# A table of 476 moves applied to the instruction order of a two-layer hybrid decoder trunk

## The chip, the cores and the metric

The kernel runs on one core of one Trainium2 chip. The metric is the device time of one execution in microseconds (us), lower is better. The core has five instruction queues that matter here: TensorE (PE in the profile, with its weight loads as PEld), VectorE (DVE), ScalarE (ACT), GpSimd (POOL) and SyncE (SP), which issues all the transfers between DRAM and on-chip memory. Each queue runs its instructions in the order in which they are written; between queues there are semaphores.

## The reference

```python
D_MODEL, SEQ, DEPTH, D_FF = 1024, 1024, 2, 2816
def reference(x, ...):
    for l in range(DEPTH):
        h = rmsnorm(x, attn_norm[l])
        c_q, c_kv, k_r, g_b, g_c, u_conv, u_pool, q_sw, k_sw, v_sw = split(h @ w_in[l])
        y_a = mla_attention(c_q, c_kv, k_r, ...)       # 4 heads, causal
        y_b = short_gated_conv(g_b, g_c, u_conv, conv_w[l])
        y_c = multiscale_pool(u_pool, ...)
        y_d = swa_sink_attention(q_sw, k_sw, v_sw, ...)  # window 128
        mixed = rmsnorm_of_each_group(y_a, y_b, y_c, y_d) * mix_norm[l]
        x = x + mixed @ w_o[l]
        h2 = rmsnorm(x, ffn_norm[l])
        gate, up = split(h2 @ w_gate_up[l])
        x = x + (silu(gate) * up) @ w_down[l]
    return rmsnorm(x, final_norm)
```

All of it is float32, with one sequence of 1024 tokens.

## The kernel before

The activations lie transposed: channels on the 128 partitions, tokens on the free axis, in two halves of 512 tokens. Each float32 operand of a matmul is split into a high part in a reduced format (`fp32r`, a cast on ScalarE, line 280) and the rest (a subtraction on VectorE, line 283), and each product is the sum of three matmuls (high x high, high x low, low x high; `mm3`, line 260). So every weight that is loaded passes through ScalarE and VectorE before TensorE can use it.

A layer has four stages, in the time of layer 0: attention and the other mixers with the input projection (0 to about 352 us), the output projection and the second norm (to about 430 us), gate and up of the FFN (to about 880 us), and the down projection (to about 1160 us); layer 1 follows in the same way.

The two products of the FFN are done as 2 x 2 blocks with seven block products instead of eight, so weights and activations are first added to one another: the weights on POOL (lines 1213 to 1215 and 1243 for gate and up, line 1532 for down), the activations on VectorE. In the FFN a step `f` computes one column block of gate and up for all tokens: it loads two pieces of `w_gu` (lines 1202 and 1204), adds and splits them, and runs seven groups of 12 or 24 matmuls into banks of PSUM. VectorE and ScalarE take the results out of the banks: line 1333 (gate = bank + snapshot), line 1321 (a snapshot of a bank, on ScalarE), line 1658 (`up`), line 1670 (the second half of the gate), line 359 (times the norm's factor), line 1453 (silu on ScalarE, followed by a product on POOL, line 1454), line 1447 (`neg_mul`, the finished activation, which reads the bank last and so gives it back to TensorE). Lines 1132, 1463 and 1465 combine finished activations, and line 1468 stores them. At some steps the weights of the down projection are also prepared (load, line 1525; sums on POOL, line 1532; store, line 1535).

In the stage between, `out_last` (line 1181) adds the output projection to the residual, and `rnorm` ends the norm: line 351 is an exponential on ScalarE, line 352 a product on VectorE, behind which TensorE starts the next product. Lines 1143, 1145 and 1153 (`combine`) prepare block sums of the activations there. In attention, line 466 is a split for the sliding-window queries and keys, line 634 the sliding-window product with the values.

The order of the instructions is not that of the code. The kernel is traced once; the class `Order` then has a planner with a cost for each kind of instruction, which simulates the five queues and puts the instructions of each queue in a row (`find`, `run`). The row is imposed on a second trace as dependencies between neighbours (`impose`). The names of tiles in the order carry a number; `u` are the slots in SBUF, `ps_` the banks in PSUM, `te`, `tn`, `tp` temporary tiles, `in_` inputs in DRAM, `ad`, `qd`, `gd` scratch in DRAM.

Of the kernel before, what the change touches and what calls it, by code (L numbers as in the profile page):

```python
# [1801 lines left out]

class Order:


# [202 lines left out]
    def banks(self, end):  # L2010
# [11 lines left out]
            given.append(b)  # L2022
        return given

    @staticmethod
    def impose(tc, traced, order):
        for ks in order.values():
            for a, b in zip(ks, ks[1:]):
                tc.add_manual_dep(
                    traced[b],  # L2030
                    traced[a].name,
                    mybir.DependencyInfo(
                        mybir.DependencyClass.NoSync, mybir.DependencyReason.DATA
                    ),
                    reason="order",
                )


def scheduled_kernel(fresh, ins_of, rounds=4):

    def trace(banks, order=None):
        nc = fresh()
        ins, out = ins_of(nc)
        with tile.TileContext(nc) as tc:
            trunk_kernel(tc, ins, out, banks)
            traced = [
                i
                for i in nc.cur_bb.bb.instructions  # L2050
                if Order.queue(i) in Order.ENGINES and i.opcode != "TilePoolBoundary"
            ]
            if order is not None:
                Order.impose(tc, traced, order)
        return nc, traced

    nc, traced = trace(None)
    plan = Order(traced, nc.dependency_edges)
    best = None
    for _ in range(rounds):  # L2060
        banks = plan.banks(plan.find()[2])
        nc, traced = trace(banks)
        plan = Order(traced, nc.dependency_edges)
        found = plan.find()
        if best is None or found[0] < best[0]:
            best = found[0], banks, found[1]
    return trace(best[1], best[2])[0]


def _constants():  # L2070
# [130 lines left out]
```

## Time and profile before

| | |
|---|---|
| median of 3 runs | 2066.03 us (2065.02 to 2066.41) |
| span of the profiled execution | 2061.2 us |
| granted clock of TensorE | 1.00, by stretches 0.99 to 1.00 |
| instructions on PE, DVE, ACT, POOL | 9422, 2443, 1743, 420 |
| moved by transfers | 302.37 MB |

The profiled execution has a span only, from its first instruction to its last; no device time of that same execution is given beside it. Its times by stages (stretch: length, then busy us and count of PE, PEld, DVE, ACT and POOL, granted clock of TensorE, mean busy share of the DMA engines, GB/s):

```profile
0.00:352.00 352.00, 348.33 (x1712) 284.49 (x1713) 302.03 (x690) 217.61 (x484) 14.11 (x28) 1.00 0.26 89
352.00:430.00 78.00, 74.20 (x323) 59.34 (x323) 70.86 (x108) 58.80 (x91) 4.11 (x2) 1.00 0.36 127
430.00:1170.00 740.00, 737.13 (x3316) 608.70 (x3315) 492.49 (x677) 296.65 (x468) 281.12 (x191) 1.00 0.50 168
1170.00:1380.00 210.00, 209.37 (x1042) 171.31 (x1041) 185.97 (x418) 140.56 (x309) 2.95 (x16) 1.00 0.23 77
1380.00:1445.00 65.00, 63.36 (x278) 51.67 (x277) 61.89 (x95) 51.59 (x80) 5.78 (x2) 1.00 0.32 113
1445.00:2061.00 616.00, 602.95 (x2760) 498.05 (x2758) 390.49 (x456) 227.38 (x317) 269.28 (x183) 0.99 0.54 183
```

To read it: the length of a stretch less the busy time of PE is the time in which TensorE did nothing there.

### The profile page before, as it was taken

Reading aid. Unit: us, or ns where it says so; the run is one execution under the profiler, and the core shown is the slowest. Engines: PE = TensorE matmul, PEld = TensorE weight load, DVE = VectorE, ACT = ScalarE, POOL = GpSimd, SP = SyncE. Lnnn points to the kernel's source line nnn. Section 1 sums busy time; section 2 is a strip of 40 time slices with the busy share of each in tenths; the row PEclk is TensorE's granted clock in tenths of the full one; section 3 lists DMA queues with packets and bytes.
Section 4 is the critical chain, followed back from the end, with each engine's and each line's share of the span. In section 5 each row is a group of like instructions: output and inputs, shape, how many; then the busy total and the mean of one; then the engine's idle time right before and its main releaser. Section 6 shows DMA issues by size and latency. Waiting matters only on the chain.

```text
span 2061.2 us, 26597 instructions
## 1 busy us (share of the span) xinstructions
PE 2035.3 (99%) x9422; PEld 1673.6 (81%) x9422; DVE 1503.7 (73%) x2443; ACT 992.6 (48%) x1743; POOL 577.3 (28%) x420
## 2 busy tenths in 40 slices
PE   9999999999999999999999999999999999999998
PEld 7887888778888888888888878888788877788887
DVE  8779979987666667655657898889866655585555
ACT  7447657753333334444433666668433333354342
POOL 0200000037777773000002000000577777710000
PEclk9999999999999999999999999999999999999999
DMA  5211223334554556766413112142455555487642
GB/s 191 90 57 46 84 78 96 137 133 168 181 175 167 189 169 235 265 220 208 140 46 124 37 42 97 61 144 94 159 169 178 178 175 170 154 302 237 204 171 96
DMA packets 142118, 302.37 MB, mean 147 GB/s; under 512 B 13856, under 2 KB 60960, under 8 KB 141984
## 3 DMA queue, kind: packets, MB, share of 16 engines
q1 hardware_dynamic: 141984, 300.66, 43.1%
q8 instruction: 74, 1.21, 0.2%
q14 instruction: 60, 0.49, 0.1%
HBM read 212.00 MB, written 87.56 MB: 145 GB/s over the span
## 4 chain that ended last, share of the span: by engine, by line
PE 68%; POOL 7%; DVE 5%; DMA 4%; issue 2%; ACT 2%; SPq 0%; DVEq 0%; POOLq 0%; ACTq 0%
PE ps_mm L260 25%; PE ps_s L260 21%; PE ps_t L260 8%; PE ps_pv L260 6%; POOL u L1532 3%; PE ps_pv L1044 2%; PE ps_t L1032 1%; DMA u<-in_w_dn 1%; POOL tp L1454 1%; DMA ad<-u 1%; POOL u L1214 1%; DVE u L283 1%; POOL u L1213 1%; ACT u L280 1%; DMA u<-in_w_gu 1%
## 5 line engine op out<-in xcount | busy, mean ns | idle before, releaser
L260 PE MATMUL ps_mm<-u,u 128*128 128x512 f32 (+1 forms) x3378 | 831.0, 390 | 3.4 <-ACT u L280 2.3
L260 PEld LDWEIGHTS ps_mm<-u,u 128*128 128x128 f32 x3378 | 615.4, 188 | 130.4 <-issue 5.3
L260 PE MATMUL ps_s<-u,u 128*128 128x512 f32 x2670 | 636.1, 390 | 5.8 <-DVE tn L352 2.3
L283 DVE TENSOR_TENSOR u<-u,u 128x1024 fp32r<-128x1024 f32 (+2 forms) x400 | 443.3, 1126 | 225.2 <-ACT u L280 173.4
L260 PEld LDWEIGHTS ps_s<-u,u 128*128 128x128 f32 x2670 | 499.5, 188 | 117.8 <-ACT tn L1321 3.9
L280 ACT CAST u<-u 128x1024 fp32r<-128x1024 f32 (+2 forms) x400 | 345.1, 881 | 505.4 <-POOL u L1215 60.1
L260 PE MATMUL ps_t<-u,u 128*128 128x512 f32 (+1 forms) x1124 | 255.3, 378 | 2.8 <-DVE u L1447 2.7
L260 PEld LDWEIGHTS ps_t<-u,u 128*128 128x128 f32 x1124 | 201.6, 188 | 45.8 <-DVE u L1447 6.5
L1454 POOL TENSOR_TENSOR tp<-tp,u 128x512 f32<-128x512 f32 x80 | 135.1, 1689 | 341.7 <-ACT tp L1453 341.7
L260 PE MATMUL ps_pv<-u,u 128*128 128x512 f32 x744 | 177.8, 390 | 1.6 <-DVE te L1658 1.0
L260 PEld LDWEIGHTS ps_pv<-u,u 128*128 128x128 f32 x744 | 139.3, 188 | 32.1 <-ACT tn L1321 1.9
L1041 POOL MEMSET u<- 128x128 f32 x32 | 5.9, 211 | 472.9 <-PE ps_pv L1044 149.3
L1453 ACT ACTIVATE tp<-tp 128x512 f32<-128x512 f32 x80 | 50.5, 631 | 155.2 <-DVE tp L359 155.1
L749 POOL TENSOR_TENSOR u<-u,u 128x512 f32<-128x512 f32 x4 | 6.0, 1509 | 380.4 <-PE ps_t L622 288.9
L1532 POOL TENSOR_TENSOR u<-u 128x352 f32<-128x352 f32 x64 | 80.5, 1259 | 31.6 <-DMA u<-in_w_dn 30.2
L280 ACT CAST u<-ps_t 128x512 fp32r<-128x512 f32 (+3 forms) x132 | 65.1, 504 | 48.1 <-PE ps_t L1032 26.7
L1532 POOL TENSOR_TENSOR u<-u,u 128x352 f32<-128x352 f32 x64 | 85.0, 1328 | 3.0
L285 ACT ACTIVATE u<-u,par 128x512 fp32r<-128x512 f32 x100 | 70.6, 717 | 28.5 <-DVE u L359 11.1
L283 DVE TENSOR_TENSOR u<-ps_t,u 128x512 fp32r<-128x512 f32 (+3 forms) x132 | 75.9, 582 | 11.1 <-ACT u L280 9.8
L286 DVE SCALAR_TENSOR_TENSOR u<-u,par,u 128x512 fp32r<-128x512 f32 x100 | 73.7, 750 | 5.9 <-ACT u L285 5.9
L324 ACT ACTIVATE tn<-u 128x512 f32<-128x512 f32 (+1 forms) x91 | 52.3, 595 | 48.6 <-DVE u L1723 42.1
L359 DVE TENSOR_TENSOR tp<-tp,u 128x512 f32<-128x512 f32 x76 | 72.5, 954 | 2.0
(208 smaller groups left out, 2359.3 us busy)
## 6 DMA issues: line engine op xcount, KB each, us to landing
u<-in_w_gu SPq DMA_DIRECT2D x92, 512.0 KB, 4.1
ad<-u SPq DMA_DIRECT2D x154, 256.0 KB, 3.9
u<-ad SPq DMA_DIRECT2D x70, 512.0 KB, 5.1
u<-in_w_dn SPq DMA_DIRECT2D x64, 352.0 KB, 3.4
qd<-u SPq DMA_DIRECT2D x64, 352.0 KB, 2.4
u<-qd SPq DMA_DIRECT2D x32, 512.0 KB, 4.7
u<-in_w_in SPq DMA_DIRECT2D x28, 512.0 KB, 3.5
u<-in_w_dn SPq DMA_DIRECT2D x24, 512.0 KB, 5.2
```

Source lines behind the costliest of these rows:

```text
L260: pe.matmul(o, w, r, start=start and k == 0 and i == 0, stop=stop and k == n - 1 and i == 2, skip_group_check=again,)
L280: a = act.copy(hi, f)
L283: dve.tensor_tensor(out=lo, in0=f, in1=rd(hi), op=ALU.subtract)
L285: a = act.activation(hi, f, AF.Copy, scale=gain)
L286: dve.scalar_tensor_tensor(out=lo, in0=f, scalar=gain, in1=rd(hi), op0=ALU.mult, op1=ALU.subtract)
L324: act.activation(q, f, AF.Square)
L359: dve.tensor_tensor(out=o, in0=a, in1=b, op=ALU.mult)
L1032: pe.transpose(p[:, b * P : (b + 1) * P], pr[b][j // 4][:, (j % 4) * P : (j % 4 + 1) * P], ident,)
L1044: pe.matmul(py[:, c0:], v_of(j, h), R.ap(s)[:, c0:], start=j == 0 and n == 0, stop=j == nj - 1 and n == 1,)
L1453: last_silu = act.activation(g, g, AF.Silu)
L1454: pool.tensor_tensor(out=g, in0=g, in1=r, op=ALU.mult)
L1532: pool.tensor_tensor(out=o, in0=a, in1=b, op=ALU.add)
```

## The change

After the planner has found its order, a table of 476 moves is applied to it, one after the other. A move `e,i,n,d` takes from queue `e` (0 PE, 1 ACT, 2 DVE, 3 POOL, 4 SP) the `n` instructions from place `i` on and puts them back `d` places later (earlier, if `d` is negative). 223 moves are for VectorE, 103 for SP, 96 for ScalarE, 29 for POOL and 25 for TensorE. 404 of them move one instruction, and 236 move by one place. The instructions, the tiles, the banks and the dependencies stay the same; the planner's costs and the choice of banks too. The table was found by search and is kept in the source.

```diff
+MOVES = (
+    "4,31,1,3 4,32,1,2 4,30,1,3 4,13,1,-2 4,12,1,-6 2,155,1,1 2,107,1,-1 2,159,1,12 4,40,1,3 "
...
+)
 class Order:
...
+    @classmethod
+    def moved(cls, order):
+        for m in MOVES.split():
+            e, i, n, d = map(int, m.split(","))
+            ks = order[cls.ENGINES[e]]
+            block = ks[i : i + n]
+            del ks[i : i + n]
+            ks[i + d : i + d] = block
+        return order
...
-    return trace(best[1], best[2])[0]
+    return trace(best[1], Order.moved(best[2]))[0]
```

Four places in the program show what this does (a row with - is where an instruction stood, with + where it stands now).

VectorE in an FFN step of layer 0, about 685 us: `ps_s_6195` is the bank that the finished activation of line 1447 reads last, line 283 is the split of a weight that a later step needs.

```order
 L1670 TENSOR_TENSOR tp_6321<-ps_mm_6267,tn_6261 128x512
 L359 TENSOR_TENSOR tp_6321<-tp_6321,u7_3957 128x512
+L1447 SCALAR_TENSOR_TENSOR u21_3801<-ps_s_6195,tp_6226 128x512
 L283 TENSOR_TENSOR u11_6384<-u31_6191,u26_6383 128x1024
-L1447 SCALAR_TENSOR_TENSOR u21_3801<-ps_s_6195,tp_6226 128x512
 L1447 SCALAR_TENSOR_TENSOR u7_3957<-te_6296,tp_6321 128x512
 L1333 TENSOR_TENSOR tp_6379<-ps_t_6349,tn_6362 128x512
```

The activation now stands ahead of the split.

VectorE in the first full FFN step of layer 1, about 1480 us: line 1658 reads the bank `ps_s_13305`.

```order
+L283 TENSOR_TENSOR u46_13338<-u39_13278,u0_13337 128x1024
 L283 TENSOR_TENSOR u22_13356<-u32_13279,u28_13355 128x1024
-L283 TENSOR_TENSOR u46_13338<-u39_13278,u0_13337 128x1024
-L1463 TENSOR_TENSOR u15_13138<-u19_13269,u15_13138 128x512
 L283 TENSOR_TENSOR u39_13391<-u17_13286,u10_13390 128x1024
 L1658 TENSOR_TENSOR te_13388<-ps_s_13305,tn_13372 128x512
-L283 TENSOR_TENSOR u27_13423<-u32_13279,u27_13423 128x512
+L1463 TENSOR_TENSOR u15_13138<-u19_13269,u15_13138 128x512
 L1670 TENSOR_TENSOR tp_13407<-ps_mm_13359,tn_13353 128x512
 L359 TENSOR_TENSOR tp_13407<-tp_13407,u30_12675 128x512
+L283 TENSOR_TENSOR u27_13423<-u32_13279,u27_13423 128x512
```

A combination of activations (line 1463) has moved behind line 1658, a split behind lines 1670 and 359, and two splits have changed places.

VectorE in the norm between attention and FFN of layer 0, about 417 us: line 352 is the norm's last step before TensorE.

```order
 L283 TENSOR_TENSOR u39_4222<-tp_4211,u39_4222 128x512
+L352 SCALAR_TENSOR_TENSOR tn_4233<-ps_pv_4229,tn_4233 128x512
 L1153 SCALAR_TENSOR_TENSOR tp_4212<-u16_2451,nffn_83,tp_4210 128x512
 L1145 SCALAR_TENSOR_TENSOR tp_4323<-u16_2451,par_75,te_4319 128x512
-L352 SCALAR_TENSOR_TENSOR tn_4233<-ps_pv_4229,tn_4233 128x512
+L283 TENSOR_TENSOR u32_4215<-tp_4210,u32_4215 128x512
 L1262 TENSOR_TENSOR u31_2542<-ps_t_4176,tn_4189 128x512
-L283 TENSOR_TENSOR u32_4215<-tp_4210,u32_4215 128x512
```

Line 352 now stands ahead of the two block sums of lines 1153 and 1145.

SP in the FFN step at about 666 us: line 1202 loads a piece of `w_gu` for a later step, line 1468 stores activations, line 1525 loads pieces of the down projection's weights.

```order
+L1468 DMA ad2_90<-u12_6182 128x512
 L1468 DMA ad3_91<-u10_6228 128x512
-L1202 DMA u31_6191<-in_w_gu 128x1024
-L1468 DMA ad2_90<-u12_6182 128x512
 L1468 DMA ad4_92<-u10_6228 128x512
 L1468 DMA ad1_89<-u12_6182 128x512
 L1468 DMA ad5_93<-u26_6229 128x512
 L1468 DMA ad6_94<-u26_6229 128x512
+L1525 DMA u26_6246<-in_w_dn 128x2x352
 L1525 DMA u10_6245<-in_w_dn 128x2x352
-L1525 DMA u26_6246<-in_w_dn 128x2x352
+L1202 DMA u31_6191<-in_w_gu 128x1024
```

The load of `w_gu` has moved behind the stores and the two other loads.

59 rows, old and new, of the table MOVES are left out of this document.

## The prediction

> **What bounds the kernel now.** I read the head of the page first, then the list of waits of TensorE, then the table by stretches, then the timeline around each of the larger waits. The head of the page:
>
> ```profile
> span 2061.2 us, 26597 instructions
> ...
> PE 2035.3 (99%) x9422; PEld 1673.6 (81%) x9422; DVE 1503.7 (73%) x2443; ACT 992.6 (48%) x1743; POOL 577.3 (28%) x420
> ```
>
> TensorE is busy for 2035.3 of 2061.2 us. The table moves instructions and takes none away, so the 2035.3 stay, and the whole prize is the 25.9 us in which TensorE does nothing. Those are named, for the most part, by the list of TensorE's waits (the instruction that waits, what it waited for: us in total, times, longest us). It has 17 rows, which add up to 18.3 us; here are 13 of them, the first and the last included:
>
> ```profile
> PE ps_t L260 <- DVE u L1447: 2.7, 7, 1.2
> PE ps_s L260 <- DVE tn L352: 2.3, 1, 2.3
> PE ps_mm L260 <- ACT u L280: 2.3, 2, 1.5
> ...
> PE ps_pv L260 <- DVE te L1658: 1.0, 1, 1.0
> PE ps_s L260 <- DVE te L1658: 1.0, 1, 1.0
> PE ps_s L260 <- DVE tp L1670: 0.9, 2, 0.5
> PE ps_pv L634 <- DVE u L283: 0.8, 1, 0.8
> PE ps_s L260 <- DVE u L1181: 0.7, 1, 0.7
> PE ps_pv L260 <- ACT tn L1321: 0.6, 1, 0.6
> ...
> PE ps_t L1032 <- ACT u L1000: 0.5, 1, 0.5
> ...
> PE ps_mm L260 <- DVE u L203: 0.3, 1, 0.3
> PE ps_s L260 <- ACT u L1271: 0.3, 1, 0.3
> PE ps_s L980 <- DVE u L283: 0.2, 1, 0.2
> ```
>
> The reader is to see that there is no single large wait: about 25 short ones, and nearly all of them on an elementwise step of VectorE (DVE) or ScalarE (ACT), not on a transfer. Whether those engines had room to do the step sooner is told by the table by stretches (stretch: length, busy us and count of PE, PEld, DVE, ACT, POOL, then granted clock, DMA share, GB/s); one stretch of attention, one of the FFN:
>
> ```profile
> 200.00:250.00 50.00, 49.48 (x241) 40.67 (x240) 48.11 (x106) 31.43 (x71) 0.35 (x2) 1.00 0.22 74
> 700.00:750.00 50.00, 50.00 (x222) 41.42 (x221) 33.40 (x38) 15.05 (x21) 35.65 (x24) 1.00 0.55 182
> ```
>
> In the FFN VectorE is idle for 16.6 of 50 us, so a wait for it there is one of order: something less urgent stood in front. In attention it is busy for 48.1 of 50 us and order can give little. The granted clock is full (1.00), so nothing is to be had from it.
>
> A wait costs slightly more than its row says, because the matmuls behind it start more slowly. Twelve undisturbed ones take 2.88 us in the FFN, twelve behind a wait 3.01 us:
>
> ```profile
> 680.83 2.88 PE L260 MATMUL ps_s<-u,u 128*128 128x512 f32 x12
> ...
> 687.60 3.01 PE L260 MATMUL ps_t<-u,u 128*128 128x512 f32 x12 [1.17 <-DVE u L1447]
> ```
>
> So I add 0.13 us for each wait removed. (A row of the timeline: start, length, engine, line, operation, tiles, count, and in brackets the idle time before it and what ended it.)
>
> **The change part by part, FFN.** The wait in the second row shows the pattern of most moves. VectorE ahead of it:
>
> ```profile
> 685.16 1.78 DVE L283 TENSOR_TENSOR u<-u,u 128x1024 fp32r<-128x1024 f32 x1 [2.25 <-ACT u L280]
> 686.86 0.68 DVE L1447 SCALAR_TENSOR_TENSOR u<-ps_s,tp 128x512 f32<-128x512 f32 x1
> ```
>
> The split of a weight (L283, 1.78 us) starts at 685.16 and the product that TensorE needs to get its bank back (L1447) only behind it, at 686.86; TensorE waits 1.17 us. The table puts L1447 ahead of that split, here and at its like in other steps. The row of L1447 has 2.7 us in seven waits: 2.7 + 7 x 0.13 = 3.6. I leave 0.4 for one of the seven at 1652 us, on whose chain I find no move: **3.2 us**. The split itself comes later by the 0.68 us of L1447. What covers that: an earlier one like it
>
> ```profile
> 645.75 1.23 DVE L283 TENSOR_TENSOR u<-u,u 128x1024 fp32r<-128x1024 f32 x1 [1.93 <-ACT u L280]
> ...
> 664.64 2.66 PE L260 MATMUL ps_s<-u,u 128*128 128x512 f32 x11
> ```
>
> ends at 646.98, and the first matmul to read its result is in the second row, 17.7 us later; if that cover were gone, each such move would cost the 0.68 us which it gives.
>
> L1658 makes TensorE wait twice, once in the first FFN step of each layer. In layer 1 VectorE has, ahead of L1658,
>
> ```profile
> 1480.43 1.77 DVE L1463 TENSOR_TENSOR u<-u,u 128x512 f32<-128x512 f32 x1
> 1482.12 2.31 DVE L283 TENSOR_TENSOR u<-u,u 128x1024 fp32r<-128x1024 f32 x1
> ```
>
> Now L1463 goes behind L1658 (the two splits ahead of these rows change places too). If the split at 1482.12 can start when L1463 has left, L1658 comes 1.7 us sooner, more than the 1.0 of the wait: 2 x (1.0 + 0.13) = **2.26 us** with its like in layer 0. L1670 waits twice for 0.9 us together; the longer (0.5, at 781 us) I see no help for, the other gives 0.4 + 0.13 = **0.53 us**. For L1321 a snapshot on ScalarE is put ahead of an activation:
>
> ```profile
> 1769.65 0.62 ACT L1453 ACTIVATE tp<-tp 128x512 f32<-128x512 f32 x1
> ```
>
> That is 0.62 against a wait of 0.6 + 0.13; between 0 and 0.73 I take **0.45**, since the activation's own reader then starts later. The FFN gives 3.2 + 2.26 + 0.53 + 0.45 = 6.4 us.
>
> The row 1482.12 also bears on what a delayed split costs: 2.31 us, against 1.23 at 645.75, the same shape. The difference, 1.08 us, comes while POOL works. [...]
>
> **Between attention and FFN.** In layer 0 lies the largest single wait, 2.3 us for L352:
>
> ```profile
> 417.17 0.61 ACT L351 ACTIVATE tn<-tn 128x512 f32<-128x512 f32 x1
> ...
> 418.61 0.68 DVE L352 SCALAR_TENSOR_TENSOR tn<-ps_pv,tn 128x512 f32<-128x512 f32 x1
> ```
>
> L352 (the end of the norm) needs L351, which ends at 417.78. Now it stands ahead of L1153 and of L1145 behind it, and can start at about 417.82 instead of 418.61: 0.79, of which I take **0.75**. The other 1.6 us of the wait are the chain before L351 and stay. VectorE then stands idle until L351 has ended, and what is behind comes about 0.4 us later. The two waits for casts on ScalarE (L280, 2.3 us, the longer 1.5) have no move that helps them: the shorter, ten us further on, should grow by those 0.4 us, and at the longer, at 1442, a swap on VectorE puts a step ahead of the chain for about one short step; between 0 and the 0.68 of such a step I take 0.5: **-0.9 us**.
>
> In the same stage the load of a gate/up weight is issued ahead of two half loads on SP, and its split moves up:
>
> ```profile
> 357.60 7.43 DMA u<-in_w_gu
> ```
>
> The load took 7.43 us and stands on the chain that ended last; L1181, which queued behind its split on VectorE, is what TensorE waits for, 0.7 + 0.13 = 0.8 us. If the loads only share the same bandwidth the gain is 0; with the issues of two half loads and their bytes out of its way it is all. I take **0.8**, since the split's cast too now stands ahead of another step of ScalarE. L1271 is put forward on ScalarE in layer 1: 0.3 + 0.13 = **0.45**. Together 0.75 - 0.9 + 0.8 + 0.45 = 1.1 us.
>
> **Attention.** The wait of L634 in layer 0 (0.8 us) is for a split that stands behind
>
> ```profile
> 94.48 1.78 DVE L466 TENSOR_TENSOR u<-te,u 64x512 fp32r<-64x512 f32 x1 [0.69 <-ACT u L464]
> ```
>
> The split of the values now goes ahead of L466's 1.78 us. That would take away all of 0.8 + 0.13, but L466 feeds the keys, and VectorE has no room here (stretch 200 to 250): between 0 and 0.93, I take **0.5**. L1000 gives **0.5** (0.6 with its restart, less a little for VectorE's full queue), L203 0.3 + 0.13 = **0.45**: 1.45 us in all.
>
> The first loads (x and w_in) change places at the start; the same bytes are needed before the first product, and I cost it at 0, within 0.1. Sum: 6.4 + 1.1 + 1.45 = 9.0 us off the span of 2061.2, so 2052.2. The median of the runs, 2066.03, lies 4.8 us above that span, and I carry this along: **2057.0 us**.
>
> **The rivals.** 0.2% of the time, 4.1 us, is about what a measurement of this kernel can tell from no change.
>
> *The waits come back elsewhere.* TensorE, ahead by some us, meets the chains that no order shortens: POOL's sums (35.65 of 50 us in the FFN), the loads, ScalarE's table load, the norms. For it: those ends set the 1.6 us left at L352 and the 2.3 of L280. Against it: the 700 to 750 stretch runs at 50.00 of 50 without one wait. Then between nothing and half of the sum remains: gain of -3 to 5 us, 2061 to 2069, most likely 2063.
>
> *More than the sum.* All 18.3 us of waits and 25 restarts at 0.13 go: 18.3 + 3.3 = 21.6. Half the way from 9 to that, 15 us, gives 2051, all of it 2044. Against it: L352 and L280 keep some 4 us.
>
> *Slower by late loads.* At eight places the load of a gate/up weight (L1202) goes three to eight places down SP's queue. One of them is issued and first read (by a sum on POOL) at
>
> ```profile
> 666.65 0.33 SPq L1202 DMA_DIRECT2D u<-in_w_gu  x1
> ...
> 681.06 1.30 POOL L1213 TENSOR_TENSOR u<-u,u 128x512 f32<-128x512 f32 x1
> ```
>
> Now it stands behind five stores and these two loads of w_dn:
>
> ```profile
> 672.46 2.28 SPq L1525 DMA_DIRECT2D u<-in_w_dn  x2
> ```
>
> They end at 674.74, so it is issued at about 675, 6 us ahead of its reader instead of 14. The median landing of such a load is less, the 7.43 us above are more:
>
> ```profile
> u<-in_w_gu SPq DMA_DIRECT2D x92, 512.0 KB, 4.1
> ```
>
> It decides once landing takes over 6 us there and the sums pass the delay on. To end slower by 4.1 us the eight places must lose 13.1, or 1.64 each, that is, land in 7.7 us each time; at 7.75 each the time is 2057 + 14 = 2071. Against it: 4.1 is the median, and the splits behind the sums have many us in hand, as shown above.
>
> [...]
>
> *The moves do not land where meant.* The order of the changed program shows L1447, L1658 and L352 where the above has them, so I give this nothing.
>
> **How the numbers follow.** Forecast (gain of 5 to 14): 0.66. Waits come back: 0.22. More than the sum: 0.07. Late loads: 0.04. Dearer splits: 0.01. Faster by over 0.2% means under 2061.9: the first and the third and a little of the second, 0.76. Slower, over 2070.2: 0.05. The rest, 0.19, lies within. The bounds of the disputed terms (L634 0 to 0.93, L1181 0 to 0.8, L280 -1.1 to 0, L1000 and L203 0 to 1.05, L1321 0 to 0.73) give 2055 to 2060 if all fall on one side; from the rivals I take the near half of "more" (2050) and of "come back" (2064): 2050 to 2064.
>
> **What would show it.** In the profile of the changed kernel TensorE's busy time should stay at 2035; the row of L1447 should be down to 0.3, both rows of L1658 gone, L352's at 1.5 to 1.6, L280's up from 2.3 to about 3, L634's and L1181's gone or under 0.3. If instead new rows of over 0.5 us stand there for POOL's sums (L1213 to L1215) or for loads of w_gu, the waits have come back elsewhere or the loads are late. I am wrong if the busy time changes, or if the waits fall as said and the span does not follow.

## The result, and the profile after

The changed kernel takes 2046.8 us (median of 4 runs, 2044.42 to 2048.04) against 2065.53 of the kernel before (4 runs); the ratio is 0.9909, with a 95% interval of 0.9897 to 0.9920. That is 18.7 us less where 9 were forecast, and below the range of 2050 to 2064. The head of the page after:

```profile
span 2043.8 us, 26551 instructions
...
PE 2025.6 (99%) x9422; PEld 1677.5 (82%) x9422; DVE 1511.1 (74%) x2443; ACT 994.4 (49%) x1743; POOL 551.7 (27%) x420
```

TensorE's idle time fell from 25.9 to 18.2 us, by 7.7, close to the forecast's 9.0 less its restarts (some 15 of 0.13). But its busy time, which the forecast held fixed, fell too, from 2035.3 to 2025.6, by 9.7 us. That is the unforeseen half. All rows of TensorE's waits after (waiting instruction, what it waited for: us in total, times, longest us):

```profile
PE ps_mm L260 <- ACT u L280: 4.0, 2, 2.0
PE ps_pv L476 <- DVE ones L134: 1.1, 1, 1.1
PE ps_s L260 <- DVE tn L352: 1.0, 1, 1.0
PE ps_s L347 <- ACT tn L346: 0.6, 1, 0.6
PE ps_s L260 <- ACT u L280: 0.5, 1, 0.5
PE ps_mm L260 <- ACT u L285: 0.5, 1, 0.5
PE ps_mm L260 <- DVE te L359: 0.4, 1, 0.4
PE ps_t L260 <- DVE tn L352: 0.4, 1, 0.4
PE ps_mm L260 <- DVE u L286: 0.3, 1, 0.3
PE ps_pv L1044 <- DVE u L283: 0.2, 1, 0.2
```

They add up to 9.0 us. The 17 rows of before add up to 16.3, not to the 18.3 of the prediction. L1447, L1658, L1670, L634 and L1181 are gone; the two large waits for L280 have grown from 2.3 to 4.0.

Since both programs run the same matmuls, each matmul of the one trace can be matched with its fellow in the other, and their starts compared ("matched starts" below). So much shorter are the stages, each measured from its own start (us):

| stage | forecast | measured |
|---|---|---|
| attention, layers 0 and 1 | 1.45 | 3.7 and 0.5 |
| between attention and FFN, layers 0 and 1 | 1.1 in both | 1.3 and -1.2 |
| gate and up of the FFN, layers 0 and 1 | 6.4 in both | 5.1 and 8.5 |
| down, and the end | 0 | 0.0 and -0.4 |
| sum | 9.0 | 17.4 |

The FFN is the largest miss, 13.5 for 6.4.

Each of these figures compares one profiled execution with one other, and carries less than its digits say. Four kernels of the experiments below (`ffn1_dve` and its three fellows) have exactly the order of the kernel before up to 1470 us. Yet their attention in layer 0 is 1.0 to 1.6 us shorter than in the profile of before, the stage behind it is between 0.6 shorter and 1.7 longer, and gate and up of layer 0 are 0.3 to 2.6 longer. Set against these four, the changed kernel's gain in the three stages would read 2.1 to 2.7, 0.7 to 3.0 and 5.3 to 7.7. Two profiles of the changed kernel agree within 0.3 us in every stage.

### What a wait costs

Undisturbed, a group of matmuls starts before the last one of the group ahead has ended. Two groups in the timeline of before, the first shown already: 680.83 + 2.88 = 683.71, and the next one starts at

```profile
683.55 2.88 PE L260 MATMUL ps_pv<-u,u 128*128 128x512 f32 x12
```

0.16 us earlier: a matmul lasts 390 ns in the records, and in an undisturbed row one starts every 227 (24 in 5.44 us on the chain that ended last). So the first 0.16 us (390 less 227 ns) by which an operand is late leave no idle time; they are booked as busy. In the wait of before that ends at 687.60, idle was 1.17 us; against its fellow after the change the same matmul lost 1.33 us, and 1.46 when the slow restart of 0.13 (3.01 less 2.88) is over. A wait costs its idle time plus 0.16 plus 0.13, that is, idle plus 0.29. A lateness of less than 0.16 costs up to 0.3 and is in no row of the list. One of these, from the timeline of before (ScalarE and TensorE, in order of start; other engines left out):

```profile
647.64 3.01 PE L260 MATMUL ps_t<-u,u 128*128 128x512 f32 x12 [0.26 <-DVE u L1447]
...
649.05 1.05 ACT L280 CAST u<-u 128x1024 fp32r<-128x1024 f32 x1 [2.80 <-POOL u L1215]
650.01 0.58 ACT L1321 COPY tn<-ps_s 128x512 f32<-128x512 f32 x1
...
650.64 1.67 PE L260 MATMUL ps_s<-u,u 128*128 128x512 f32 x6
```

The group at 650.64 starts exactly when the one before it ends (647.64 + 3.01 = 650.65), so no idle time is shown, but it is 0.16 late: it needs the snapshot L1321, which stands behind a cast that has waited for POOL's sum L1215. The same place after the change:

```profile
640.96 2.88 PE L260 MATMUL ps_t<-u,u 128*128 128x512 f32 x12
641.22 0.59 ACT L1321 COPY tn<-ps_s 128x512 f32<-128x512 f32 x1 [1.66 <-PE ps_s L260]
...
641.70 1.05 ACT L280 CAST u<-u 128x1024 fp32r<-128x1024 f32 x1
...
643.68 2.20 PE L260 MATMUL ps_s<-u,u 128*128 128x512 f32 x9
```

The snapshot is ahead of the cast, done by 641.81, and the next group overlaps by 0.16 again. Summed over the starts of all matmuls, the time lost against the pace of 227 ns (us):

| | before | after |
|---|---|---|
| waits with idle time, those under 0.15 us included: number, loss, idle in it | 29, 23.4, 14.6 | 7, 10.0, 6.0 |
| places late without idle time: number, loss | 21, 4.4 | 12, 2.1 |
| start, end, and products of whole float32 | 13.3 | 11.6 |
| lateness under 0.1 us a place | 7.2 | 6.8 |
| all | 48.2 | 30.4 |

The waits at the start and at the end are in the third row. The first row of before has 8.8 us over its idle time in 29 waits, 0.30 each. In the first row of after, 1.6 of the 10.0 us is a stretch at half clock (last section).

### The profile page after: what moved, and what is told of

It reads as the page before. It is cut to its first block, busy times and chain, and to the rows that moved or that the text cites. A ratio compares the mean times of both kernels' runs of the same rounds, so it can differ in the third digit from the quotient of the medians.

```text
span 2043.8 us, 26551 instructions
## 1 busy us (share of the span) xinstructions
PE 2025.6 (99%) x9422; PEld 1677.5 (82%) x9422; DVE 1511.1 (74%) x2443; ACT 994.4 (49%) x1743; POOL 551.7 (27%) x420
## 4 chain that ended last, share of the span: by engine, by line
PE 94%; DVE 3%; ACT 1%; issue 1%; DMA 0%; POOL 0%; SPq 0%; DVEq 0%; ACTq 0%
PE ps_mm L260 37%; PE ps_s L260 29%; PE ps_t L260 11%; PE ps_pv L260 8%; PE ps_pv L1044 2%; PE ps_t L1032 1%; PE ps_s L978 1%; PE ps_s L980 1%; PE ps_s L979 1%; PE ps_s L573 1%; PE ps_s L850 1%; PE ps_pv L634 1%; PE ps_t L622 1%; PE ps_t L343 1%; DVE u L286 0%
## 5 line engine op out<-in xcount | busy, mean ns | idle before, releaser
L283 DVE TENSOR_TENSOR u<-u,u 128x1024 fp32r<-128x1024 f32 (+2 forms) x400 | 448.2, 1141 | 175.9 <-ACT u L280 137.8
L280 ACT CAST u<-u 128x1024 fp32r<-128x1024 f32 (+2 forms) x400 | 344.9, 881 | 395.4 <-PE ps_s L260 62.7
L1454 POOL TENSOR_TENSOR tp<-tp,u 128x512 f32<-128x512 f32 x80 | 127.6, 1595 | 342.2 <-ACT tp L1453 342.2
L280 ACT CAST u<-ps_t 128x512 fp32r<-128x512 f32 (+3 forms) x132 | 65.2, 503 | 49.9 <-PE ps_t L1032 25.6
L283 DVE TENSOR_TENSOR u<-ps_t,u 128x512 fp32r<-128x512 f32 (+3 forms) x132 | 75.9, 580 | 10.6 <-ACT u L280 9.5
L1243 POOL TENSOR_TENSOR u<-u 128x512 f32<-128x512 f32 x38 | 73.3, 1930 | 27.9 <-DVE u L283 27.9
L1532 POOL TENSOR_TENSOR u<-u,u 128x352 f32<-128x352 f32 x64 | 75.9, 1185 | 7.6 <-DMA u<-in_w_dn 4.7
L1532 POOL TENSOR_TENSOR u<-u 128x352 f32<-128x352 f32 x64 | 75.2, 1175 | 8.9 <-DMA u<-in_w_dn 7.9
```

Source lines behind the costliest of these rows:

```text
L280: a = act.copy(hi, f)
L283: dve.tensor_tensor(out=lo, in0=f, in1=rd(hi), op=ALU.subtract)
L1243: pool.tensor_tensor(out=q4, in0=q4, in1=F.ap(self.raw[1] + 1), op=ALU.add)
L1454: pool.tensor_tensor(out=g, in0=g, in1=r, op=ALU.mult)
L1532: pool.tensor_tensor(out=o, in0=a, in1=b, op=ALU.add)
```

## The experiments

There were two theories at first. A: a wait costs its idle time plus 0.29, and short ones are not shown. B: it costs its idle time plus 0.13, and the rest of the gain has other sources, such as the loads. Where a result below is turned into us, "by the ratios" uses the medians of the runs, and "by the spans" or "by matched starts" the one profiled execution of each kernel.

### One part alone, and all but that part

`neg_first_alone`: in the order of before, 14 moves in place of the 476 (`2,815,1,1` is the first), each of the form

```diff
-L283 split 128x1024
 L1447 (reads the bank)
+L283 split 128x1024
```

> The kernel before, with one part of the change alone: at the 14 FFN steps where L1447 stood directly behind a 128x1024 split (L283) on VectorE, the two change places; nothing else moves. Theory A (a wait of TensorE costs its idle time plus 0.16 us that the profile books as busy, since a matmul lasts 390 ns but one can start every 227, plus 0.13 us of slower restart, and waits under 0.16 us cost time without any idle time): in the profile of before eight of these sites have waits that cost 5.1 us of TensorE's time in all (2.7 us of it idle) and six of them are followed by a wait for a snapshot (L1321) that costs 0.3 and shows no idle time. A expects 5 to 7 us less span than before, of which idle time explains only 2.7 and TensorE's busy time falls by 2.3 to 4. Theory B (a wait costs its idle time plus 0.13, and the unforeseen half of the gain comes from elsewhere, such as the loads on SP): 3.6 us less span, busy time down by at most 1.

Measured: 2061.79 us, ratio 0.9987 (0.9977 to 0.9996), which is 2.7 us less than before (0.8 to 4.7). The spans of the two profiled executions are 2061.0 and 2061.2, so there it is 0.2. A's 5 to 7 lies outside both figures; B's 3.6 lies within the first. L1447 is gone from the list of waits, and there stand instead

```profile
PE ps_s L260 <- ACT tn L1321: 3.9, 8, 0.6
...
PE ps_pv L260 <- ACT tn L1321: 1.0, 2, 0.6
```

In the timeline the first of the places above now reads

```profile
649.76 1.06 ACT L280 CAST u<-u 128x1024 fp32r<-128x1024 f32 x1 [2.82 <-POOL u L1215]
650.73 0.57 ACT L1321 COPY tn<-ps_s 128x512 f32<-128x512 f32 x1
...
651.35 1.43 PE L260 MATMUL ps_s<-u,u 128*128 128x512 f32 x5 [0.32 <-ACT tn L1321]
```

TensorE comes sooner and waits for the snapshot, which has not moved. This is the forecast's first rival, *the waits come back elsewhere*. At some places the exchange also makes a wait where there was none: at 573.77 us of before TensorE had no idle time, and now it waits 0.54 us for a snapshot. POOL's sum L1215, on which the cast ahead of that snapshot depends, starts there at 571.67 instead of 570.42.

`neg_behind_split`: the changed kernel with 14 moves added that put each of these splits directly ahead of L1447 again.

> The changed kernel with that one part undone: at the same 14 FFN steps the split is put directly ahead of L1447 again, all other moves stay. Theory A: 5 to 7 us more span than the changed kernel, TensorE's busy time up by 2.3 to 4, the waits for L1447 back with about 2.7 us. Theory B: 3.6 us more span, busy time up by at most 1.

Measured: 2053.34 us, ratio to before 0.9944 (0.9929 to 0.9958), against 0.9909 for the changed kernel: 7.2 us more, and the intervals do not touch. The span is 2052.1, 8.3 us more than the changed kernel's.

```profile
PE 2029.3 (99%) x9422; PEld 1677.0 (82%) x9422; DVE 1507.7 (73%) x2443; ACT 994.3 (48%) x1743; POOL 549.0 (27%) x420
...
PE ps_t L260 <- DVE u L1447: 4.2, 6, 1.3
```

Busy time rises by 3.7 and idle time by 4.6. Busy time tells A from B here: A has 2.3 to 4, B at most 1. Of the 8.3 us, 1.3 are lost ahead of the FFN of layer 0, where no split was moved; 5.5 and 1.6 lie in gate and up of the two layers, near A's 5 to 7. This is not an exact undoing, since three of the six waits for L1447 (the one of 1.3 us among them) stand at places where before had none: the splits now stand among casts that have moved too. So the part is worth 2.7 us alone and 7.2 within the whole by the medians, 0.2 and about 7 by the profiled executions: less alone, though by how much less stays open.

`no_sp_moves` leaves out queue 4, as shown; `dve_act_only` has `if e not in (1, 2):` there and leaves out all but ScalarE and VectorE:

```diff
             e, i, n, d = map(int, m.split(","))
+            if e == 4:
+                continue
```

> The changed kernel without the 103 moves on SP (transfers are issued in the old order), all others kept. Theory A: the SP moves carry the wait for L1181 (0.7 idle + 0.29 = 1 us) and perhaps part of the start, so at most 2 us more span than the changed kernel. Theory B with the loads as the other half: 8 to 9 us more.

> The changed kernel with the moves on VectorE and ScalarE alone (319 of 476); TensorE, POOL and SP keep the old order. Theory A: nearly all TensorE waits were for these two engines, so the gain stays but for 1 to 3 us: span 2045 to 2047. Theory B: half of the gain goes, span 2052 to 2055.

Measured: 2047.37 us (ratio 0.9918, 0.9903 to 0.9933; span 2045.6) and 2057.73 us (0.9962, 0.9947 to 0.9977; span 2056.6). B's loads as the other half of the gain are out: without SP's moves 1.8 us of span are lost, where B had 8 to 9. (2.8 are lost before the FFN of layer 0, where L1181 is waited for again, and 1.5 won in layer 1, where no stretch at half clock came, of which more below.)

```profile
PE ps_t L260 <- DVE u L1181: 1.1, 2, 0.8
```

But A's 1 to 3 us for the other three queues together was wrong: it was 12.8 by the spans, 10.9 by the ratios. By matched starts the 12.8 lie at the start (1.9), before the FFN of layer 0 (5.9) and in that FFN (3.3), for the most part, and 4 of the 12.8 are more stretches at half clock (below). In the FFN of layer 1 only 0.3 is lost: VectorE's and ScalarE's moves carry that stage.

`no_pool_moves` and `no_pe_moves` leave out queue 3 and queue 0 by the same lines.

> The changed kernel without the 29 moves on POOL. The kernel with VectorE's and ScalarE's moves alone was 11 us slower than the changed one, the one without SP's only 0.6 by the runs' medians (1.8 by the spans), so 9 to 10 us should lie with POOL's or TensorE's moves or with two of the three together. If POOL's moves carry it: 5 to 10 us more span than the changed kernel, in the FFN of layer 0. If SP's with TensorE's or a lowered clock (four stretches at 0.5 were seen with VectorE's and ScalarE's moves alone, one in the changed kernel, each 1 to 1.6 us): at most 2 us more.

> The changed kernel without the 25 moves on TensorE. By the spans the SP moves alone are worth 1.8 us, POOL's 4.6 (1.6 of it one more stretch at half clock), and all three together 12.8. If the three added up, TensorE's would be worth 4 to 6 us, in attention and at the start (at the start 1.3 us, at the two places in attention where L343's products go ahead 0.4 each). If they are mostly worth something together with SP's and POOL's: 1 to 2.5 us.

Measured: 2048.01 us (0.9915, 0.9900 to 0.9930; span 2048.4) and 2049.6 us (0.9926, 0.9911 to 0.9941; span 2048.3). Against the span of the changed kernel that is 4.6 and 4.5 us, each with one stretch at half clock more; by the ratios it is 1.2 and 3.5. Without POOL's moves 3.9 of it lie between attention and FFN of layer 0 and 0.5 in the FFN of layer 1; without TensorE's 2.5 lie in that first place and nothing in either FFN. One by one the three queues' moves are worth 10.9 us and together 12.8 by the spans; by the ratios 6.6 and 10.9, each ratio with an interval of about 3 us to either side. That they need one another is therefore not shown.

### Links in series

Theory C: TensorE waits for the later of two steps, L1447 on VectorE and the snapshot on ScalarE. `snap_first_alone` exchanges 17 snapshots with the cast ahead of them (`1,527,1,-1` is the first); `neg_and_snap` has these and the 14 of L1447; `neg_snap_cast` also puts 11 casts behind the silu, or the silu and the snapshot, that followed (`1,554,1,2` is one).

> The kernel before with one part of the ScalarE moves alone: at 17 places of the FFN the snapshot of a bank (L1321) that stood directly behind a cast of 128x1024 (L280) changes places with it; nothing else moves. Theory C (formed after the first four runs): the 14 L1447 on VectorE and these snapshots on ScalarE are two links behind one another; TensorE waits for the later of the two, so moving L1447 alone only hands the wait to the snapshot, whose cast waits for POOL's sum L1215. C expects of this half alone 2 to 3.5 us less span than before (the snapshot waits of the profile of before, 8 of them for 3.2 us of TensorE time), with the L1447 waits left at about 2.7 us. Rival: POOL's sums are what is late, and no order of ScalarE helps: within 1 us of before.

> The kernel before with both halves: the 14 L1447 ahead of their splits and the 17 snapshots ahead of their casts, nothing else. Theory C: both links gone, 5.1 + 3.2 = 8.3 us less span than before (7 to 10), more than the sum of the halves alone (0.2 and 2 to 3.5), and L1447 and L1321 nearly vanish from TensorE's waits. Rival (POOL late): 2 to 3 us less, with waits for other steps in their place.

> The kernel before with three parts of the change: the 14 L1447 ahead of their splits, the 17 snapshots (L1321) ahead of their casts, and at 11 places of ScalarE's order in the FFN a cast of 128x1024 (L280) put behind the silu (L1453), or the silu and the snapshot, that followed it. With the first two alone the span didn't fall (2062.5), since new waits of up to 1.9 us stood there for snapshots behind casts that themselves waited for a transfer. Theory C2 (TensorE waits for the latest of several links, and all must move before any time is won): with the third link gone the waits for L1321 fall from 4.8 us to under 1.5, and the FFN stages get 4 to 8 us shorter than in the kernel before. Rival C3 (the loads and stores themselves are late, whatever the order on ScalarE): less than 1.5 us shorter.

Measured: 2065.0 us (0.9995, 0.9986 to 1.0004), 2062.39 us (0.9986, 0.9976 to 0.9995) and 2059.19 us (0.9971, 0.9962 to 0.9980). By the ratios these are 1.0, 2.9 and 6.0 us less than before. The second is C's failure, which had 7 to 10; two links were not all. In its timeline:

```profile
714.54 1.04 ACT L280 CAST u<-u 128x1024 fp32r<-128x1024 f32 x1 [7.23 <-DMA ad<-u]
715.49 0.62 ACT L1453 ACTIVATE tp<-tp 128x512 f32<-128x512 f32 x1
...
716.02 0.57 ACT L1321 COPY tn<-ps_s 128x512 f32<-128x512 f32 x1
...
716.64 2.97 PE L260 MATMUL ps_s<-u,u 128*128 128x512 f32 x8 [1.85 <-ACT tn L1321]
```

Another cast, waiting for a store to end, holds up the silu and the snapshot behind it. In before it started at 711.04. The third kernel moves such casts. Its profiled execution gains 2.0 and 1.2 us in the two FFN stages, less than C2's 4 to 8; the ratio's 6.0 (4.1 to 7.8) for the whole kernel lies within them, so the profile alone would judge it too hard. The waits for L1321 are down to 2.0 us (C2: under 1.5), and new ones of 1.5 us each stand for L1670 and for one more snapshot.

What was still open was which moves belong together. Four kernels take the new order in the FFN of layer 1 alone, from VectorE (98 places differ), ScalarE (27), both, or all five queues; everywhere else the old order is put back:

```diff
+    KEEP = {'DVE': (1894, 2147), 'Activation': (1277, 1450)}
...
+        old = {e: list(ks) for e, ks in order.items()}
         for m in MOVES.split():
...
+        for e, ks in order.items():
+            a, b = cls.KEEP.get(e, (0, 0))
+            ks[:a], ks[b:] = old[e][:a], old[e][b:]
```

This is the one with both; a queue that `KEEP` does not name keeps the old order throughout.

> The kernel before with the changed order on VectorE alone, in the FFN stage of layer 1 alone (gate and up, 1480 to 1860 us; 98 places differ), everything else as before. In the changed kernel this stage is 8.5 us shorter. Theory C2 (links on VectorE and ScalarE in series): 1 to 3.5 us of it, with waits for snapshots (L1321) in place of L1447. Rival D (VectorE's order is all that counts, the narrow version of it tried before was too small a part): 7 to 8.5.

> The same with ScalarE's order alone (27 places differ). C2: 0 to 2 us shorter, the waits for L1447 and L1658 stay. D: 0.

> The same with VectorE's and ScalarE's order together. C2: 7 to 8.5 us shorter, more than the sum of the two alone. If POOL or SP are needed as well (they differ at 41 and 44 places in this stage): under 5.

> The same with the changed order of all five engines in that stage (TensorE's doesn't differ there). 8 to 9 us shorter by the span, since the stage starts from the same point.

| | ratio to before | that stage shorter by (matched starts) |
|---|---|---|
| VectorE | 0.9976 (0.9966 to 0.9987) | 2.8 |
| ScalarE | 1.0001 (0.9992 to 1.0011) | 2.0 |
| both | 0.9959 (0.9944 to 0.9973) | 7.4 |
| all five | 0.9959 (0.9945 to 0.9974) | 7.8 |

The stage's rows of TensorE's waits: before,

```profile
PE ps_t L260 <- DVE u L1447: 1.3, 5, 0.3
PE ps_s L260 <- DVE te L1658: 1.0, 1, 1.0
PE ps_pv L260 <- ACT tn L1321: 0.6, 1, 0.6
PE ps_s L260 <- DVE tp L1670: 0.4, 1, 0.4
```

with VectorE's order alone,

```profile
PE ps_s L260 <- ACT tn L1321: 2.9, 3, 2.0
```

and with both,

```profile
PE ps_s L260 <- DVE te L1658: 0.4, 1, 0.4
```

What these lists show is the handing over. With VectorE's order alone L1447, L1658 and L1670 are gone, and TensorE waits 2.9 us in three waits for snapshots, where it had waited 0.6 in one; with ScalarE's order added, these are gone too. C2 was wrong on ScalarE's order alone: the waits for L1447 did not stay but fell from 1.3 to 0.6 us, while the one for L1658 grew from 1.0 to 2.1.

That the two orders are worth more together than one by one is likely, but not shown. By matched starts 2.8 and 2.0 add up to 4.8, and together it is 7.4; but VectorE's alone includes a stretch at half clock of 1.6 behind its wait of 2.0, without which the sum would be 6.4, and executions of one order differ by as much as the 1.0 to 2.6 that remain. By the ratios it is 5.0 us (2.7 to 7.0) and -0.2 (-2.3 to 1.7) alone and 8.5 (5.6 to 11.6) together. Rival D (7 to 8.5 for VectorE alone) lies above both figures, and at the edge of that interval.

The 7.4 can be counted out by A's price: in before this stage has 3.5 us idle in ten waits and six late places without idle, 16 x 0.29 = 4.6; together 8.1, less the 0.4 + 0.29 that is left at L1658, is 7.4.

### The waits that grew

In the changed kernel the two casts L280 between attention and FFN are the longest waits. `cast_first` adds `1,488,1,-1 1,1256,1,-1`, which puts both ahead of the silu and its table load; `cast_first_l1` adds only the second. `after_again` is the changed kernel once more:

> The changed kernel with two more moves on ScalarE: in each layer, between attention and FFN, the cast (L280) of the third weight sum goes ahead of the silu (L1453) and of the load of its table, behind which it stood. In the changed kernel these two casts are TensorE's longest waits (4.0 us idle in two), and after the second the granted clock is 0.5 for about 3.4 us (8 matmuls at 427 instead of 227 ns, 1.6 us). If the cast's data are there in time and the silu can be later, theory A and C expect 4.0 + 2 x 0.29 + 1.6 = 6 us less span, 3 to 6 with what the silu, later by 1.05 us, gives back; if the data come late or the silu's readers are waited for, no change within 1 us.

> The changed kernel once more, to stand beside the next run on the same chip. 2044 to 2048 us. On the lowered clock: in the profiles so far waits of 1.9 to 2.4 us of TensorE were followed by a stretch at half clock in 7 of 18 cases, so it may or may not show after the waits at 423 and 1431 us; each stretch would be 7 to 8 matmuls at 427 ns, 1.4 to 1.6 us lost.

> The changed kernel with the cast put ahead of the silu in layer 1 only. With both layers the span stayed (2044.0 against 2043.8): in layer 0 the wait went over to the split of an activation combination behind the later silu, and 1.5 us were lost, in layer 1 a wait of 2.0 us became one of 0.9 and 1.7 us were won, most of it because no stretch at half clock followed. Theory: layer 1 alone keeps that gain, 1 to 2 us less span than the changed kernel if that has the stretch at half clock, about 0.2 if it has not.

Measured: 2045.46 us (0.9903, 0.9888 to 0.9918), 2045.64 (0.9907, 0.9892 to 0.9922), 2045.79 (0.9909, 0.9893 to 0.9926), in the order of the texts above: no difference between the three. The two waits for L280 are gone in the first, and TensorE waits soon after for what comes behind the silu:

```profile
427.22 0.69 DVE L359 TENSOR_TENSOR u<-ps_s,tp 128x512 f32<-128x512 f32 x1 [2.31 <-POOL tp L1454]
...
428.56 0.49 PE L260 MATMUL ps_mm<-u,u 128*128 128x512 f32 x1 [1.16 <-DVE u L283]
```

By matched starts the third wins 1.7 us in layer 1, where no stretch at half clock followed, and loses 1.6 in layer 0, where one did now.

## Why the prediction was wrong, by its own steps

- "So I add 0.13 us for each wait removed" is the step that failed: a wait removed is worth its idle time plus 0.29, and the list of waits does not hold the places that are late by under 0.16 us. With it fell "so the 2035.3 stay": TensorE's busy time fell by 9.7 us. That is made of 22 waits fewer at about 0.29 each (6.4), places without idle (2.3), start and float32 products (2.3, of which 0.6 came back as idle time) and smaller lateness (0.4), less the 1.6 of half clock.
- FFN, 6.4 forecast, 13.5 measured: the waits named were the right ones and went. The idle time in the two stages was 6.4 us (2.9 and 3.5), and there were 23 late places, 15 with idle time and 8 without; at 0.29 each they make 6.7, together 13.1. The eleven waits that were costed would have given about 8.2 at the right price; the eight places without idle time give 2.3, and the rest are waits that were left out or costed low.
- Three readings of the prediction were wrong. The rows of TensorE's waits add up to 16.3, not 18.3, so the 21.6 of "more than the sum" should have been 19.6. None of the seven waits for L1447 is at 1652 us: the wait there is one of 0.14 for a snapshot, and all seven went, so the 0.4 was held back for nothing. And the 1.08 us by which a split gets dearer does not tell a split beside POOL from one without: POOL works beside the split at 645.75 too (last section).
- The pattern (L1447 ahead of a split) was named rightly as a move, but counting each wait as won by the move at its own place was unsound: alone the 14 moves give 0.2 us between the profiled executions and 2.7 by the medians, where 3.2 was counted, and TensorE's waits for L1321 stand in place of those for L1447. That in the whole table the sum of the idle times comes out owes something to the other moves, which were not costed.
- Attention, 1.45 forecast, 4.2 measured. The start gave 0.6 where 0 was set, L634 1.1 for 0.5, L203 0.6 for 0.45, a move on TensorE (L343's products at 183 us) 0.4 that had not been costed; L1000 gave hardly anything, since L283 is waited for there now. The 1.1 of L634 can't be put down to its move: four kernels with the old order in attention (`neg_snap_cast`, `ffn1_act`, `ffn1_dve_act`, `ffn1_all`) show no such wait either.
- Between attention and FFN, 1.1 forecast, 0.1 measured. L352 fell from 2.3 to 1.0, more than the 0.75, though a wait of 0.4 for it is new in layer 1. L280 rose by 1.7 instead of 0.9, and a lowered clock of 1.6 us came on top.
- The rival "more than the sum" (0.07) is where the time came out, but not by its mechanism. Its 2051 to 2044 held the result, and that is luck: it was put low because L280 and L352 keep some 5 us, which they did, and what made up for it was the busy time, of which it says nothing.
- "Late loads" did not come about: the load that was at 666.65 is issued at 667.24, and its reader L1213 starts at 672.49, 5.3 us later and without a wait. "Dearer splits", with a chance of 0.01, neither: no run shows that the moved splits take 1.08 us more each. The 257 splits of 128x1024 take 1.36 us each on the mean before and after, VectorE's busy time rose by 7.4 us, and no new wait is for a split in the FFN.

## What to carry to other kernels

Price a wait of a busy engine from the starts of its instructions, not from the idle time in the list: match one undisturbed group with one disturbed and take the whole shift, and look for groups that begin exactly at the end of the one before. When an instruction stands late behind another, ask what the waiting engine needs next from the other engines: if that is late by nearly as much, a move gains nothing by itself. Here one part was worth 2.7 us alone and 7.2 within the whole, and between two profiled executions it showed as 0.2 alone; a trial of it by itself would have undervalued it. Before a stage that is one or two us shorter is put down to a move, look at a second execution of the same order, or at a kernel that has the same order in that stage: here such executions differed by up to 2.6 us.

## What the runs showed of the hardware

After some waits of TensorE of about 2 us the granted clock was 0.50 (half clock). In the changed kernel, between attention and FFN of layer 1 (windows: length, then busy us and count of PE, PEld, DVE, ACT, POOL, granted clock, DMA share, GB/s):

```profile
1432.00:1434.00 2.00, 0.18 (x1) 0.18 (x2) 0.76 (x2) 1.99 (x4) 1.09 (x1) 1.00 0.10 41
1434.00:1435.00 1.00, 1.00 (x3) 0.77 (x4) 0.79 (x2) 0.81 (x2) 0.18 (x1) 0.58 0.00 0
1435.00:1436.00 1.00, 1.00 (x4) 0.80 (x3) 1.00 (x2) 0.00 (x0) 0.00 (x0) 0.50 0.23 88
1436.00:1437.00 1.00, 1.00 (x4) 0.81 (x3) 1.00 (x3) 0.00 (x0) 0.00 (x0) 0.50 0.46 174
1437.00:1438.00 1.00, 1.00 (x4) 0.75 (x4) 0.97 (x2) 0.00 (x0) 0.00 (x0) 0.72 0.00 0
```

Eight matmuls start 420 to 427 ns apart, where 227 is undisturbed: 1.6 us lost in 3.4. A wait of 1.98 us in layer 0 of the same run had no such stretch. Over all 18 profiles of this case, 17 of the 27 waits of 1.8 to 2.4 us idle were followed by one, and none of the single waits of 1.3 to 1.6 us. (The expectation of `after_again` has 7 of 18; the ten profiles that it could go by show 8 of 15.) Two more stretches, both in `dve_act_only`, follow pairs of shorter waits: 0.96 and 0.55 us at the start, 1.15 and 0.70 at 369 us. What decides whether a wait of this length has the stretch or not, no run shows.

Sums on POOL that started beside a split on VectorE took about twice as long. In before the 29 sums of 128x352 (L1532) that start during a split of 128x1024 take 1.88 us on the mean, the 13 without any work of VectorE beside them 0.94. One beside the split of 645.75, and its fellow after the change without a split beside it:

```profile
645.85 1.93 POOL L1532 TENSOR_TENSOR u<-u 128x352 f32<-128x352 f32 x1
```

```profile
639.16 0.94 POOL L1532 TENSOR_TENSOR u<-u 128x352 f32<-128x352 f32 x1
```

The split itself took 1.23 us there, as long as splits of this size beside which POOL does nothing (1.22 on the mean of 153 in before). At 1482.12, where a sum already ran when the split started, the split took 2.31 (the 78 such splits in before: 1.66 on the mean, 1.22 to 2.37). POOL's busy time fell from 577.3 to 551.7 us with the same 420 instructions, while VectorE's rose from 1503.7 to 1511.1.
